# An encoder block on one core: 234 products on zeros in front of the opening, with moving rows read straight on, in turn from two or more places, at several distances and widths

## The chip, the cores and the metric

The kernel runs on one core of a Trainium2 chip. The metric is the device time of one execution in microseconds; the figure for a kernel is the median of its runs. Two runs of the kernel before took 1772.62 and 1772.77 us, a median of 1772.69 us.

## What is computed

One layer of a bidirectional encoder block on 256 tokens of 2048 channels, fp32, batch 1. Cut to what matters:

```
proj = h @ w_in                                # 2048 -> all inputs of the branches and gates
q, k, v, r, af, ab, hy_u, gate_logits = split(proj)
y_gla = gla_branch(q, k, v, r, af, ab, ...)    # chunked gated linear attention, both directions
y_hy = hyena_branch(hy_u, ...)                 # short conv, long filters from a small network, two gates
merged = g0 * (y_gla @ w_gla_o) + g1 * (y_hy @ w_hy_o)
h = layernorm(ALPHA * h + merged @ w_out)
h = layernorm(ALPHA * h + square(relu(h @ w_ff1)) @ w_ff2)
```

Nearly all of the work is products of the 256 tokens with large weight matrices, which are streamed from HBM once.

## The kernel before

Each weight block arrives as fp32 (a `raw` tile, 1 MB) and is split by `split_hi_lo` (L104, L105) into a high part, rounded by ScalarE, and a low part, the rest, by VectorE. Activations are split in the same way, so that a product of fp32 accuracy is made of three products of rounded parts (high by high, high by low, low by high). `channel_products` (L193, L197) keeps weights stationary and moves 512 columns (high and low part of the 256 tokens, side by side in memory) past the high weights, then 256 columns past the low ones. `token_half` (L250 to L252) and the MLP's second matrix (L1378 to L1380) keep activations stationary and move 512 columns of weights. The moving columns of each of these products lie next to each other in memory.

The kernel begins with the *opening*: the first five blocks of `w_in` and x itself come together in eleven pieces (`PIECES`, issued on SyncE's queue at L317), each is split on ScalarE and VectorE (L104, L105, L349, L352, L354), and TensorE takes it slice by slice of the contraction, 16 in all: five products of 512 columns (L337) and four of 256 (L339) each. In front of it `wu`, 512 columns of zeros, is written by VectorE (L310), and two fp32 products on it (L313, tile `warm`, four rows in the profile) keep TensorE at work until the first piece has been split. After the opening come the blocks of q and k, with the filter network's products (L425, L426, tile `mlp`) and the filters' transforms (L469 to L473, L378 to L382) between them, then the other projections, the branches, the output projection and the MLP.

The order of instructions on each engine is set by a scheduler that simulates a timeline of the whole program (`schedule_with_timeline_sim=True`); `tc.keep_in_program_order` pins an instruction to its place in the program's order. The filter work has no fixed place: it is put where the simulated timeline has room. Each engine works its queue in order.

The lines around the change:

```
wu = xp.tile([P, 512], F32, tag="wu", name="wu")
nc.vector.memset(wu, 0.0)
pw = psum_side("warm")
for _ in range(2):
    MM(pw, wu[:, 0:P], wu, start=True, stop=True)
```

Of the kernel before, what the change touches and what calls it, by code (L numbers as in the profile page):

```python
# [10 lines left out]
F32R = mybir.dt.float32r  # L11
# [5 lines left out]
P = 128  # L17
# [21 lines left out]
PIECES = tuple((k, 1) for k in range(6)) + tuple((k, 2) for k in range(6, KT, 2))  # L39

TWO_PI = 2.0 * math.pi
RED_C1 = 6.28125
RED_C2 = float.fromhex("0x1.fb4p-10")
RED_C3 = TWO_PI - RED_C1 - RED_C2
MAGIC = 1.5 * 2.0 ** 23
# [4 lines left out]
def block_kernel(  # L50
# [25 lines left out]
    nc = tc.nc  # L76
# [20 lines left out]
    def psum_main(name):  # L97
        return mmp.tile([P, 512], F32, tag="mm", name=name)

    def psum_side(name):  # L100
        return sdp.tile([P, 512], F32, tag="sd", name=name)

    def split_hi_lo(hi, lo, src):
        return (nc.scalar.copy(hi, src),  # L104
                nc.vector.tensor_tensor(lo, src, hi.bitcast(F32), op=ALU.subtract))  # L105
# [45 lines left out]
    def weight_half(n, h, by_channel=False):  # L151
        i = low_turn[0] % 3
        low_turn[0] += 1
        lo = (base, wp, wp)[i].tile([P, D // 2 + 8], F32R, tag=f"wlo{i}", bufs=1, name=f"wlo{n}_{h}")
        return (wp.tile([P, D // 2], F32R, tag="whi", bufs=3, name=f"whi{n}_{h}"),
                lo[:, 0:D // 2] if by_channel else lo[:, 8:])
# [140 lines left out]
    with tc.tile_pool(name="xp", bufs=1) as xp, tc.tile_pool(name="xq", bufs=1) as xq:  # L297
        def units(pool, tag, n, **kw):
            t = pool.tile([P, n, OPENING * P], F32R, tag=tag, name=f"open_{tag}", **kw)
            return lambda a, b: t[:, a:b].rearrange("p k (b j) -> p k b j", b=OPENING)  # L300

        pieces = {}
        for k0, n in PIECES[::-1]:
            if k0 < 10:
                pieces[k0] = xp.tile([P, n, KROW], F32, tag=f"xw{k0}", name=f"xw{k0}")
            else:
                raw = wp.tile([P, D], F32, tag="raw", bufs=3, name=f"xw{k0}")
                pieces[k0] = raw[:, 0:n * KROW].rearrange("p (k c) -> p k c", k=n)
        wu = xp.tile([P, 512], F32, tag="wu", name="wu")
        nc.vector.memset(wu, 0.0)  # L310
        pw = psum_side("warm")
        for _ in range(2):
            MM(pw, wu[:, 0:P], wu, start=True, stop=True)  # L313

        fetched[0] = OPENING
        for k0, n in PIECES:
            nc.sync.dma_start(pieces[k0], first[k0 * P:(k0 + n) * P, :].rearrange("(p k) c -> p k c", k=n))  # L317

        u_y, u_g, u_k, u_q, u_x = (units(base, "yT", 12), units(qp, "G", 6), units(qp, "k", 3), units(qp, "q", 2),
                                   units(xq, "sp", 3))  # L320
        places = {6: (u_y(6, 8), u_y(8, 10)), 8: (u_y(10, 12), u_g(0, 2)), 10: (u_g(2, 4), u_g(4, 6)),
                  12: (u_k(0, 2), u_q(0, 2))}
        for i in range(3):
            t = weight_half(-1, i, True)
            places[i] = [v[:, 0:OPENING * P].rearrange("p (k b j) -> p k b j", k=1, b=OPENING) for v in t]
            places[3 + i] = (u_y(2 * i, 2 * i + 1), u_y(2 * i + 1, 2 * i + 2))
        places[14], places[15] = (u_k(2, 3), u_x(0, 1)), (u_x(1, 2), u_x(2, 3))

        def part_of(kt, part):
            k0 = kt if kt in places else kt - 1  # L330
            return places[k0][part][:, kt - k0]

        def products(kts, b, part):
            for kt in kts:
                w = part_of(kt, part)[:, b]
                if part == 0:
                    MM(open_ps[b], w, xT[:, kt], start=(kt == 0), stop=(b == 0 and kt == KT - 1))  # L337
                elif b:
                    MM(open_ps[b][:, 0], w, xT[:, kt, 0], start=False, stop=(kt == KT - 1))  # L339

        turned = False
        for k0, n in PIECES:
            raw = pieces[k0]
            kts = range(k0, k0 + n)
            split_hi_lo(xT[:, k0:k0 + n, 0], xT[:, k0:k0 + n, 1], raw[:, :, 0:L])
            w = raw[:, :, L:].rearrange("p k (b j) -> p k b j", b=OPENING)

            def split(hi, lo, w, first=0):
                nc.scalar.copy(hi, w)  # L349
                if first == 0:  # L350
                    low = hi[:, :, 0, 96:]
                    nc.vector.tensor_tensor(low, w[:, :, 0, 96:], low.bitcast(F32), op=ALU.subtract)  # L352
                bs = slice(1 - first, None)
                nc.vector.tensor_tensor(lo[:, :, bs], w[:, :, bs], hi[:, :, bs].bitcast(F32), op=ALU.subtract)  # L354

            if k0 == 0:
                hi, lo = places[0]
                for bs in (slice(0, 3), slice(3, OPENING)):
                    split(hi[:, :, bs], lo[:, :, bs], w[:, :, bs], bs.start and 1)
            elif k0 == 14:  # L360
                for i in range(n):
                    split(places[k0 + i][0], places[k0 + i][1], w[:, i:i + 1])
            else:
                split(places[k0][0], places[k0][1], w)
            if k0 + n == KT:
                for b in range(OPENING):
                    for part in (0, 1):
                        products(kts, b, part)
            else:
                for part in (1, 0) if turned else (0, 1):  # L370
                    for b in range(OPENING):
                        products(kts, b, part)
                turned = not turned and k0 >= 6 and k0 < 12
# [42 lines left out]
    def filt_layer(l):  # L416
        def run():
            mw, mc, g = fst["mw"], fst["mc"], fst["g"]
            with tc.high_priority():
# [9 lines left out]
                n = fp.tile([P, L], F32, tag="ng", name=f"mlpn{l}")  # L429
                nc.vector.tensor_scalar(n, a, 1.0 / TWO_PI, MAGIC, op0=ALU.mult, op1=ALU.add)  # L430
                nc.vector.tensor_scalar(n, n, -MAGIC, None, op0=ALU.add)
                for cst in (RED_C1, RED_C2, RED_C3):
                    nc.vector.scalar_tensor_tensor(a, n, -cst, a, op0=ALU.mult, op1=ALU.add)
# [86 lines left out]
    for i in range(2 * NCH):  # L520
        c, o = divmod(i, 2)
        n = 4 + (i * 21) // 15
# [1021 lines left out]
    ps = psum_main("w2_33_0")  # L1544
# [38 lines left out]
    with tc.high_priority(), tc.issue_after(done.ins):  # L1583
        add_ff(pss[1][:, 0:256], 1, 1792, 256, last=True)
        mv = ep.tile([P, 2], F32, tag="mv", bufs=2, name="mvl")
        nc.vector.bn_aggr(mv, st2[:, 1])
        y, t, v, rs = (ep.tile([P, 1], F32, tag=f"fin{i}", name=f"fin{i}") for i in range(4))
# [160 lines left out]
```

## Time and profile before

| | |
|---|---|
| median of the runs | 1772.69 us |
| the profiled execution, its own time | 1773.26 us |
| its span, first to last instruction | 1771.4 us |
| mean granted TensorE clock | 0.999 |
| TensorE (PE) busy, instructions | 1763.8 us, 8771 |
| VectorE (DVE) busy | 1460.9 us |
| ScalarE (ACT) busy | 1048.4 us |
| DMA, mean over the span | 241 GB/s |

Times within the profile are counted from the start of the span. A row of the timeline gives start, length, engine, line, operation, output<-inputs, form and count; in brackets it has how long the engine was idle before and what ended that. A row of a group gives the count, then busy time and mean duration of one, then idle time before. PE's products overlap at their ends, so that a row's length is longer than the distance to the next start. PEld is TensorE's weight load, beside PE.

### The profile page before, as it was taken

To read this page: it belongs to the slowest core of one execution; us is meant where nothing else is said; L and a number is where in the kernel's file an instruction comes from. 1 tells how busy PE (TensorE), PEld (TensorE's weight loads), DVE (VectorE), ACT (ScalarE), POOL (GpSimd) and SP (SyncE) were. 2 spreads that over 40 slices of the span, in tenths; PEclk is the share of its full clock that TensorE was granted. 3 is DMA by queue.
4 is the path that set the end of the run, shared out by engine and by line. 5 is a ranking of instruction groups with operands and counts; after the bars stand their busy time and mean duration, and the time that the engine had idled before them with its cause. 6 is when DMAs were issued, how large, how long until landed. Compare 5 with 4: busy or idle time off the path is not lost.

```text
span 1771.4 us, 23597 instructions
## 1 busy us (share of the span) xinstructions
PE 1763.8 (100%) x8771; PEld 1490.0 (84%) x8771; DVE 1460.9 (82%) x1899; ACT 1048.4 (59%) x1446; POOL 186.5 (11%) x243
## 2 busy tenths in 40 slices
PE   9999999999999999999999999999999999999998
PEld 7888888888888888888888889888888888888886
DVE  6789996777688888888845558889999999999998
ACT  6587876787344444444444446666766666666653
POOL 1001111000110101021000000011111111111100
PEclk9999999999999999999999999999999999999999
DMA  8678888634796868797555664688878788888864
GB/s 329 230 252 265 290 258 257 199 141 173 262 299 222 279 232 273 232 287 256 192 192 187 264 247 165 207 267 253 258 242 277 241 251 256 269 249 247 267 207 168
DMA packets 87299, 427.13 MB, mean 241 GB/s; under 512 B 9800, under 2 KB 14296, under 8 KB 45584
## 3 DMA queue, kind: packets, MB, share of 16 engines
q1 hardware_dynamic: 47664, 336.35, 51.5%
q0 software_dynamic: 30560, 67.38, 18.3%
q10 hardware_dynamic: 8960, 21.89, 3.5%
q8 instruction: 69, 1.13, 0.3%
q14 instruction: 46, 0.38, 0.1%
HBM read 382.12 MB, written 12.06 MB: 223 GB/s over the span
## 4 chain that ended last, share of the span: by engine, by line
PE 96%; DVE 3%; issue 1%; ACT 0%; DVEq 0%
PE f L193 13%; PE f L197 6%; PE w L1379 5%; PE w L1380 5%; PE w L1378 5%; PE g L251 3%; PE g L252 3%; PE ux L251 3%; PE ux L252 3%; PE g L250 3%; PE ux L250 3%; PE k L193 2%; PE r L251 2%; PE r L252 2%; PE v L251 2%; PE v L252 2%
## 5 line engine op out<-in xcount | busy, mean ns | idle before, releaser
L104 ACT CAST whi<-raw 128x1024 fp32r<-128x1024 f32 x360 | 377.8, 1054 | 401.0 <-PE ux L252 86.7
L105 DVE TENSOR_TENSOR wlo<-raw,whi 128x1024 fp32r<-128x1024 f32 x360 | 438.2, 1222 | 158.1 <-ACT whi L104 154.2
L193 PE MATMUL f<-hT,whi 128*128 128x512 f32 x984 | 244.3, 391 | 0.0
L193 PEld LDWEIGHTS f<-hT,whi 128*128 128x128 f32 x984 | 180.2, 188 | 35.0
L1236 DVE TENSOR_TENSOR wlo<-fraw,whi 128x1024 fp32r<-128x1024 f32 x112 | 136.9, 1223 | 13.5 <-ACT whi L1239 9.8
L197 PEld LDWEIGHTS f<-hT,wlo 128*128 128x128 f32 x984 | 123.8, 188 | 5.2
L1239 ACT CAST whi<-ring 128x1024 fp32r<-128x1024 f32 x56 | 59.0, 1054 | 113.9 <-DVE ring L1236 113.9
L1299 POOL DMA_DIRECT2D ring<-wblk x56 | 48.6, 868 | 726.3 <-DVE ring L1236 719.9
L197 PE MATMUL f<-hT,wlo 128*128 128x256 f32 x984 | 124.9, 279 | 0.0
L1239 ACT CAST whi<-fraw 128x1024 fp32r<-128x1024 f32 x112 | 117.6, 1050 | 0.0
L1239 ACT CAST b_h<-ring 128x1024 fp32r<-128x1024 f32 x112 | 87.9, 834 | 22.3 <-PE w L1380 21.6
L251 PE MATMUL g<-wlo,xT 128*128 128x512 f32 x256 | 100.1, 391 | 0.0
L251 PE MATMUL ux<-wlo,xT 128*128 128x512 f32 x256 | 99.9, 390 | 0.0
L252 PE MATMUL ux<-whi,xT 128*128 128x512 f32 x256 | 99.9, 390 | 0.0
L252 PE MATMUL g<-whi,xT 128*128 128x512 f32 x256 | 99.8, 390 | 0.0
L250 PE MATMUL g<-whi,xT 128*128 128x512 f32 x256 | 92.2, 390 | 0.0
L250 PE MATMUL ux<-whi,xT 128*128 128x512 f32 x256 | 89.2, 389 | 0.0
L1236 DVE TENSOR_TENSOR ring<-ring 128x512 f32<-128x512 f32 x112 | 77.2, 689 | 1.9
L1236 DVE TENSOR_TENSOR b_l<-ring,b_h 128x1024 fp32r<-128x1024 f32 x56 | 68.4, 1222 | 8.1 <-ACT b_h L1239 8.0
L1236 DVE TENSOR_TENSOR wlo<-ring,whi 128x1024 fp32r<-128x1024 f32 x56 | 68.6, 1225 | 2.1 <-ACT whi L1239 0.3
L1236 DVE TENSOR_TENSOR fa<-ring,fa 128x1024 fp32r<-128x1024 f32 x56 | 68.3, 1220 | 0.0
L1300 POOL DMA_DIRECT2D ring<-ring x56 | 67.2, 1201 | 0.0
(529 smaller groups left out, 4257.8 us busy)
## 6 DMA issues: line engine op xcount, KB each, us to landing
raw<-wblk SPq DMA_DIRECT2D x188, 1024.0 KB, 5.1
fraw<-wblk SPq DMA_DIRECT2D x56, 1024.0 KB, 4.9
ring<-wblk SPq DMA_DIRECT2D x56, 1024.0 KB, 7.0
ring<-wblk POOLq DMA_DIRECT2D x56, 256.0 KB, 4.4
ring<-ring POOLq DMA_DIRECT2D x56, 256.0 KB, 5.2
conv_sb<-conv_rows SPq DMA_DIRECT2D x12, 1024.0 KB, 8.7
w<-w4s ACTq DMA_DIRECT2D x16, 512.0 KB, 5.1
Td<-T POOLq DMA_DIRECT2D x32, 256.0 KB, 5.3
```

The costliest lines, as they stand in the source:

```text
L104: return (nc.scalar.copy(hi, src), nc.vector.tensor_tensor(lo, src, hi.bitcast(F32), op=ALU.subtract))
L105: nc.vector.tensor_tensor(lo, src, hi.bitcast(F32), op=ALU.subtract))
L193: MM(ps[:, :, ts], hi[:, js], act[:, kt, :, ts], start=(kt == 0 and opens), stop=(kt == KT - 1))
L197: MM(ps[:, 0, ts], lo[:, js], act[:, kt, 0, ts], start=False, stop=False)
L250: order(MM(pss[tb], sh, wh, start=(kt == ends[0]), stop=False))
L251: order(MM(pss[tb], sh, wl, start=False, stop=False))
L252: order(MM(pss[tb], sl, wh, start=False, stop=(kt == ends[1])))
L1236: return pin(nc.vector.tensor_tensor(dst, a, b, op=op))
L1239: return pin(nc.scalar.copy(hi, src))
L1378: pin(MM(ps, sh, wh, start=(p == begin), stop=False))
L1379: MM(ps, sh, wl, start=False, stop=False)
L1380: pin(MM(ps, sl, wh, start=False, stop=(p == end - 1)))
```

## The change

A new function, `side_by_side`, is called between the two products of the warm-up and the opening. It makes a tile `both` of 2560 fp32 columns (rounded form) in the pool `xq`, fills it with zeros by five ScalarE copies of `wu`, and issues 38 groups of products on it: two groups with plain moving rows, 35 forms, and one more plain group. A group has six products, the three last forms (two kinds of rows by turns) eight. All write the bank of the warm-up, each opens and closes its own sum, and all are pinned in program order. Nothing reads what they write.

```
+def side_by_side(tc, nc, pool, ps, zero):
+    both = pool.tile([P, 2560], F32R, tag="both", name="both")
+    for i in range(5):
+        tc.keep_in_program_order(nc.scalar.copy(both[:, i * 512:(i + 1) * 512], zero))
+
+    def st(d, n=P, step=1, first=1536):
+        at = first - d // 4
+        return both[:, at:at + n * step].rearrange("p (a b) -> p a b", b=step)[:, :, 0]
+
+    def rows(n, apart, count=2):
+        t = both[:, 0:512 * 2]
+        if apart * count >= n:
+            return t[:, 0:apart * count].rearrange("p (a b) -> p b a", a=count)[:, 0:n]
+        return both[:, 0:n * count].rearrange("p (a b) -> p b a", a=count)
+
+    mv = both[:, 0:512]
+    kinds = [mv] + [rows(256, s) for s in (256, 264, 288, 320, 384, 512)]
+    kinds += [mv.rearrange("p (h a b) -> p h b a", h=2, a=2), rows(128, 128, 4), rows(64, 64, 8),
+              mv.rearrange("p (a b c) -> p b a c", a=2, c=2), mv.rearrange("p (a b c) -> p b a c", a=2, c=4),
+              mv.rearrange("p (a b c) -> p b a c", a=2, c=8)]
+    forms = [[(st(0), m)] for m in kinds]
+    two = rows(256, 256)
+    forms += [[(st(d), two)] for d in range(32, 256, 32)]
+    forms += [[(st(0, 64), two)], [(st(0, step=2), two)]]
+    low = rows(128, 128)
+    forms += [[(st(d), low)] for d in range(0, 256, 32)]
+    forms += [[(st(0), rows(128, 256))], [(st(0), mv[:, 0:256])]]
+    halves = kinds[7]
+    forms += [[(st(0), two), (st(0), low)], [(st(0), halves), (st(0), low)], [(st(32), two), (st(32), low)]]
+    for form in [[(st(0), mv)]] * 2 + forms + [[(st(0), mv)]]:
+        for i in range(8 if len(form) > 1 else 6):
+            s, m = form[i % len(form)]
+            tc.keep_in_program_order(
+                nc.tensor.matmul(ps[0:s.free_size(), 0:m.free_size()], s, m, start=True, stop=True))
+
...
         for _ in range(2):
             MM(pw, wu[:, 0:P], wu, start=True, stop=True)
+        side_by_side(tc, nc, xq, pw, wu)
```

`st(d)` are the stationary 128 columns, which begin d bytes ahead of column 1536 (64 columns wide in one form, every second column in another). `rows(n, apart, count)` takes one word from each of `count` places that lie `apart` words from each other, then the next word of each, and so on: n x count columns. The counts, by how the moving row is read:

| moving row | products of 512 columns | products of 256 columns |
|---|---|---|
| straight on (`mv`) | 24 | 6 |
| two, four or eight neighbours, then from the other half (`c=2`, 4, 8) | 6, 6, 6 | |
| single words in turn from two places | 108 | 66 |
| single words in turn from four and from eight places | 6, 6 | |
| sum | 162 | 72 |

The instruction counts are the same apart from that; the scheduler's simulated timeline, and with it the order of the filter work, has changed. Three places follow. First the start of PE's queue, before and now; `warm` is the bank of the warm-up, `open_91` to `open_95` the sums of the opening, `whi-1_0` the high part of its first weights:

```order
L313 MATMUL warm<-wu 128x512 x2
L337 MATMUL open_91<-xT,whi-1_0_135 128x512
L337 MATMUL open_92<-xT,whi-1_0_135 128x512
L337 MATMUL open_93<-xT,whi-1_0_135 128x512
L337 MATMUL open_94<-xT,whi-1_0_135 128x512
```

```order
L350 MATMUL warm<-wu 128x512 x2
L77 MATMUL warm<-both 128x512 x132
L77 MATMUL warm<-both 64x512 x6
L77 MATMUL warm<-both 128x512 x6
L77 MATMUL warm<-both 128x256 x60
...
L77 MATMUL warm<-both 128x512 x6
L375 MATMUL open_91<-xT,whi-1_0_375 128x512
L375 MATMUL open_92<-xT,whi-1_0_375 128x512
```

The 234 products stand between the warm-up and the opening's first product, which was second in the queue before; the dots stand for the 24 products of the three mixed forms.

Then the start of ACT's queue, before and now; `xT` is the high part of x, `xw_112` the first piece:

```order
L104 ACT_TABLE_LOAD
L104 CAST xT<-xw_112 128x256
L349 CAST whi-1_0_135<-xw_112 128x384
L349 CAST whi-1_0_135<-xw_112 128x256
L104 CAST xT<-xw_111 128x256
```

```order
L47 ACT_TABLE_LOAD
L47 CAST both<-wu 128x512 x5
L141 CAST xT<-xw_112 128x256
L387 CAST whi-1_0_375<-xw_112 128x384
L387 CAST whi-1_0_375<-xw_112 128x256
L141 CAST xT<-xw_111 128x256
```

The five copies into `both` stand in front of the first split; the rest of the opening's splits keep their order.

Last the place in PE's queue, behind the opening, where the first layer of the filter network (`mlp`, its input `gx`) stands between the products of q, before and now:

```order
L193 MATMUL q_0_701<-xT,whi_0_533 128x512 x8
L197 MATMUL q_0_701<-xT,wlo_0_532 128x256 x8
L197 MATMUL q_0_701<-xT,wlo_1_536 128x256 x8
L193 MATMUL q_0_701<-xT,whi_1_537 128x512 x3
L425 MATMUL mlp_388<-gx_385,mlp_ws 128x256
L193 MATMUL q_0_701<-xT,whi_1_537 128x512 x5
L193 MATMUL q_1_797<-xT,whi_0_632 128x512 x7
L426 MATMUL mlp_388<-gx_385,mlp_ws 128x256
```

```order
L230 MATMUL q_0_941<-xT,whi_0_773 128x512 x8
L234 MATMUL q_0_941<-xT,wlo_0_772 128x256 x7
L463 MATMUL mlp_628<-gx_625,mlp_ws 128x256
L234 MATMUL q_0_941<-xT,wlo_0_772 128x256
L234 MATMUL q_0_941<-xT,wlo_1_776 128x256 x5
L464 MATMUL mlp_628<-gx_625,mlp_ws 128x256
L234 MATMUL q_0_941<-xT,wlo_1_776 128x256 x3
L230 MATMUL q_0_941<-xT,whi_1_777 128x512 x8
```

The two products of the network's first layer have moved forward, from the last quarter of this block and the one behind it into its second and third quarter, and stand closer to each other.

## The prediction

> **What bounds the kernel now.** I read the page first, then the waits of PE, then PE's timeline of the opening. The page:
>
> ```profile
> span 1771.4 us, 23597 instructions
> PE 1763.8 (100%) x8771; PEld 1490.0 (84%) x8771; DVE 1460.9 (82%) x1899; ACT 1048.4 (59%) x1446; POOL 186.5 (11%) x243
> PEclk9999999999999999999999999999999999999999
> PE 96%; DVE 3%; issue 1%; ACT 0%; DVEq 0%
> ```
>
> PE is busy over the whole span, at the full granted clock, and is 96% of the chain that ended last. A busy PE could still hide short gaps, so the second view asks what PE waited for:
>
> ```profile
> engine line waited for: us in total, times, longest us
> PE warm L313 <- DVE ones_sb L375: 1.5, 1, 1.5
> PE w L251 <- DVE wr L105: 0.3, 1, 0.3
> PE w L250 <- DVE zr L1236: 0.3, 1, 0.3
> PE lo L1598 <- DVE fin L1592: 0.2, 1, 0.2
> ```
>
> That is the whole list: 1.5 us before PE's first product and 0.8 us later. There is no pocket of waiting in which added products could disappear, and none that a PE arriving later would find already over. The third view is PE's timeline (start, length, line, out<-in, form, count):
>
> ```profile
> 1.50 3.78 PE L313 MATMUL warm<-wu 128*128 128x512 f32 x4 [1.50 <-DVE ones_sb L375]
> 4.93 2.50 PE L337 MATMUL open<-xT,whi-1_0_135 128*128 128x512 f32 x5
> 7.23 0.80 PE L339 MATMUL open<-xT,wlo-1_0_134 128*128 128x256 f32 x4
> 8.06 1.42 PE L337 MATMUL open<-xT,whi-1_1_137 128*128 128x512 f32 x5
> ...
> 11.41 1.31 PE L337 MATMUL open<-xT,open_yT 128*128 128x512 f32 x5
> ...
> 16.30 2.46 PE L337 MATMUL open<-xT,open_yT 128*128 128x512 f32 x10
> ...
> 32.49 1.99 PE L193 MATMUL q<-xT,whi 128*128 128x512 f32 x8
> 34.32 2.03 PE L197 MATMUL q<-xT,wlo 128*128 128x256 f32 x16
> 36.19 3.82 PE L193 MATMUL q<-xT,whi 128*128 128x512 f32 x16
> 39.85 2.03 PE L197 MATMUL q<-xT,wlo 128*128 128x256 f32 x16
> ```
>
> Products overlap at their ends, so the price of one is the distance between starts. Sixteen products of 512 columns take 39.85 - 36.19 = 3.66 us, **0.229 us each**; sixteen of 256 take 36.19 - 34.32 = 1.87 us, **0.117 us each**. The opening runs from 4.93 to 32.49, 27.56 us for sixteen slices of the contraction. Three slices in its middle take 16.30 - 11.41 = 4.89 us, 1.63 us each, so sixteen would take 26.1 us. The missing 1.5 us lies at its start: the first five products stand 0.46 us apart ((7.23 - 4.93) / 5), and the second slice waits a little for its splitting.
>
> **The change, part by part.** It adds 234 products to PE between the warm-up (L313) and the first product of the opening (L337), all on zeros and all into the bank of the warm-up: 162 of 512 moving columns and 72 of 256. Nothing that the kernel needs depends on them, but PE works in order, so the whole opening stands behind them. ACT gets five copies of 128x512 in front of its first split. No DMA is added and none removed.
>
> *Where the added products start.* These rows carry it (ACT's, then the last split of the opening on DVE):
>
> ```profile
> 0.74 1.28 ACT L104 ACT_TABLE_LOAD   x1 [0.74 <-PEq L1740]
> 3.84 0.41 ACT L104 CAST xT<-xw 128x256 fp32r<-128x256 f32 x1 [1.81 <-DMA xw<-first]
> 13.63 0.62 ACT L104 CAST xT<-xw 128x512 fp32r<-128x512 f32 x1 [1.15 <-DMA xw<-first]
> 24.73 0.69 DVE L354 TENSOR_TENSOR open_sp<-xw,open_sp 128x512 fp32r<-128x512 f32 x1
> ```
>
> The table load ends at 2.02 and a copy of this size takes 0.62 us, so the fourth of the copies, which holds the first weights, ends at about 4.5, and the fifth at 5.1. The warm-up holds PE until about 4.93 anyway: the products start there, with no new wait. The first split of x goes from 3.84 to 5.1, 1.3 us late. I cost that at nothing: its cover is the added products, more than 40 us of them. Without that cover it would cost the 1.3 us.
>
> *The part whose price is known.* If every column came at the price of the rows above, the sum is 162 x 0.229 + 72 x 0.117 = 37.1 + 8.4 = 45.5 us. The five slow products at the start of dense work are now five of the added ones: 5 x (0.46 - 0.229) = 1.2 us more. The opening behind them finds its first splits done and gives back its 1.5 us. **Net +45.2 us.**
>
> *The part whose price is not in the trace.* Every product of the kernel before reads its moving columns from adjacent words. Of the added ones 186 do not: 120 of 512 columns and 66 of 256 take one word here, the next one 256 to 2048 bytes further on, and so on in turn. Of the rest, 24 of 512 and 6 of 256 read straight on, and 18 of 512 take two, four or eight neighbours before they jump; those I price as adjacent (for the six with two neighbours that is a guess worth 1.2 us at most). For the price of a jump I bound by the other engines that take fp32 words from the same memory, from the groups of the first 33 us (last number before the second bar: mean ns of one):
>
> ```profile
> L104 ACT CAST whi<-raw 128x1024 fp32r<-128x1024 f32 x3 | 3.1, 1049 | 3.8 <-PE open L339 2.0 <-DMA raw<-wblk 1.9
> L104 ACT CAST xT<-xw 128x256 fp32r<-128x256 f32 x6 | 2.4, 406 | 4.1 <-DMA xw<-first 3.8
> L105 DVE TENSOR_TENSOR wlo<-raw,whi 128x1024 fp32r<-128x1024 f32 x3 | 3.6, 1223 | 3.4 <-ACT whi L104 3.4
> L105 DVE TENSOR_TENSOR xT<-xw,xT 128x256 fp32r<-128x256 f32 x6 | 2.5, 422 | 4.7 <-ACT xT L104 4.7
> ```
>
> From 256 to 1024 words ACT takes (1049 - 406) / 768 = 0.84 ns a word, DVE (1223 - 422) / 768 = 1.04 ns. PE takes one in 0.229 / 512 = 0.45 ns, about half of ACT's. The lower bound is that a jump costs PE nothing: 0.229 and 0.117 stay. The middle bound is ACT's pace: 0.43 us for 512 columns and 0.215 for 256. The upper one is DVE's: 0.534 and 0.267. (That a jump should help is the last rival.) I take ACT's pace. PE is the only engine of the trace that takes more than one word in 0.84 ns, and in every row that shows it the words are neighbours; where nothing can come along with a word, the fastest pace at which any row here takes words is ACT's. The extra is 120 x (0.43 - 0.229) + 66 x (0.215 - 0.117) = 24.1 + 6.5 = 30.6 us.
>
> [...]
>
> *Behind the opening.* Scheduling by a simulated timeline has also moved rows of the filter work. The earliest place where PE could wait for it is the first layer of the filter network:
>
> ```profile
> 46.25 0.41 DVE L423 TENSOR_TENSOR gx<-emb_sb,gx 64x256 fp32r<-64x256 f32 x1
> 47.94 0.28 PE L425 MATMUL mlp<-gx,mlp_ws 128*128 128x256 f32 x1
> ```
>
> Before, the low part of its input is ready 14.2 us after the opening's end at 32.49, and the first product comes at 15.4 us. Now the first product stands about 13.6 us of PE work behind that end and the second, which alone needs the low part, at 14.5. DVE's row for the low part has moved up too. What is queued behind is the rest of the q and k products, so a wait here would count in full; I put it at 0, with 1 us either way. Everything later keeps its distance from the opening: weight splits wait for buffers that PE frees, and so shift with it.
>
> **The sum.** Net +45.2 and +30.6 make +75.8 us. The span goes from 1771.4 to 1847.2. The profiled execution took 1773.26 us, so 1849.1 for it; the median of the runs is 0.57 us lower, 1772.69, which gives **1848.5 us**.
>
> **The rivals.**
>
> *A jump costs nothing* (24%), or the rows do not jump on the chip as they do in the code. PE then takes every column in 0.45 ns: +45.2, **1817.9 us**. For it speaks that no row shows an engine losing anything to a pattern of addresses; against it that PE's pace is twice ACT's and has never been seen without neighbours.
>
> *Only some jumps cost* (13%): the price hangs on the distance between the two places, or on how many are read in turn, and about half of the 186 products pay. 45.2 + 15.3 = +60.5, about **1833 us**. For it speaks only that distances can differ in what they collide with; the trace has no row for or against.
>
> *A jump costs more than a word at DVE's pace* (9%): three of PE's steps a column, 0.69 us for 512 and 0.35 for 256, extra 55.3 + 15.4 = 70.7, in all +115.9, about **1889 us**. Nothing in the trace takes words that slowly, which is why it is small.
>
> *Two places are read at once* (3%). This is the one that ends on the other side: two streams in turn would bring two columns per step, 0.115 and 0.058 us. The jumping products would save 120 x 0.114 + 66 x 0.059 = 17.6 us against 45.2, leaving +27.6, **1800.3 us**, which is within 2%. It decides once the 234 products and what hangs on them cost under 35.4 us, 2% of 1772.69. Against it: in the q products above, PE reads neighbours at 0.45 ns and gains nothing from lying side by side; nothing goes faster.
>
> **How the numbers follow.** The forecast has 51%; with the five cases that is 100%. The range 1814 to 1867 takes in the forecast, free jumps (1817.9), the half case (1833) and DVE's pace (120 x 0.305 + 66 x 0.15 = 46.5 instead of 30.6, so 1864.4), with some 3 us for waits that the new order could bring or take; left out are the dearest and the cheapest case, 12%. About 2%, or 35 us, can be told from no change here. Faster by over 2%: 0, since added work has no wait to remove. Within 2%: 0.03, the last rival. Slower by over 2%: 0.97, the rest.
>
> **What would show it.** In PE's timeline the added products form one piece on L77 that starts at about 4.9 us; it should last about 77 us by the forecast, 47 if jumps are free, 62 by the half case. Inside it the first products after the slow five should stand 0.23 us apart, the ones that take two words in turn 0.43, those with four or eight neighbours 0.23 again, and weights at other distances should change little. ACT's first split should come at about 5.1 us without PE noticing, and the opening should take 26.1 us instead of 27.6. Were the difference in time far from the length of that piece, the argument that nothing hides it would be wrong; were the piece 77 us with the loss in other groups than the jumping ones, the price would be right for a wrong reason.

## The result and the profile after

The changed kernel takes 1819.71 us (median of 1819.09 and 1820.33), against 1772.69 before: 47.0 us more, a ratio of 1.0263 (95% interval 1.0238 to 1.0288). It is slower by over 2% and inside the range, but 29 us below the predicted 1848.5 and close to the 1817.9 us of the first rival, by which a jump costs nothing.

PE's timeline of the changed kernel, cut to the warm-up, the added piece, the opening's first products and the first of q (start, length, line, out<-in, form, count):

```profile
1.50 3.78 PE L350 MATMUL warm<-wu 128*128 128x512 f32 x4 [1.50 <-DVE ones_sb L413]
4.29 47.78 PE L77 MATMUL warm<-both 128*128 128x512 f32 x234
51.91 1.31 PE L375 MATMUL open<-xT,whi-1_0_375 128*128 128x512 f32 x5
53.06 0.63 PE L377 MATMUL open<-xT,wlo-1_0_374 128*128 128x256 f32 x4
...
77.88 1.99 PE L230 MATMUL q<-xT,whi 128*128 128x512 f32 x8
```

The piece lasts from 4.29 to 51.91, 47.6 us, where 77 were forecast and 47 is the free-jump case. The opening follows without a wait and takes 77.88 - 51.91 = 25.97 us (26.1 predicted, 27.56 before), its first five products now 0.23 us apart. The end of the opening has moved from 32.49 to 77.88, by 45.4 us; from there to the end of the span it is 1817.0 - 77.88 = 1739.1 us, against 1771.4 - 32.49 = 1738.9. So the whole difference is made before the first product of q, and nothing is given back behind it. PE's waits say the same:

```profile
PE warm L350 <- DVE ones_sb L413: 1.5, 1, 1.5
PE g L288 <- DVE wlo L142: 1.0, 1, 1.0
PE w L288 <- DVE wr L142: 0.3, 1, 0.3
PE w L287 <- DVE zr L1274: 0.3, 1, 0.3
```

One wait of 1.0 us, in the gates, is all that the new order brought; the first layer of the filter network, named as a risk, has none. ACT's first split came at 4.64 us instead of 5.1 (five copies back to back took 2.69 us, not 3.1), and nobody waited for it:

```profile
2.04 2.69 ACT L47 CAST both<-wu 128x512 fp32r<-128x512 f32 x5
4.64 0.40 ACT L141 CAST xT<-xw 128x256 fp32r<-128x256 f32 x1
```

Inside the piece the prices are not what any of the cases said. The rows below are stretches of the changed kernel, each from the first start of one set of groups to the first start of the next. After the two ends stand the stretch in us, PE's busy time and count, the granted clock, the DMA's share and its GB/s; the count includes the last product of the set before, and here and there one more, which reach in:

```profile
6.75:9.46 2.72, 2.72 (x13) 1.00 1.04 401
9.46:18.53 9.06, 9.06 (x43) 1.00 1.02 423
18.53:20.22 1.69, 1.69 (x7) 1.00 0.98 402
20.22:23.22 3.00, 3.00 (x7) 1.00 0.35 85
23.22:25.20 1.98, 1.98 (x7) 1.00 1.03 418
25.20:28.17 2.97, 2.97 (x13) 1.00 0.95 367
28.17:39.83 11.66, 11.66 (x55) 1.00 0.24 93
39.83:45.86 6.03, 6.03 (x55) 1.00 0.00 0
45.86:46.59 0.73, 0.73 (x8) 1.00 0.00 0
```

| reading of the moving row | products | us each |
|---|---|---|
| straight on, 512 columns | 12 | 0.227 |
| single words from two places in turn, seven kinds | 42 | **0.216** |
| from four places | 6 | 0.282 |
| from eight places | 6 | 0.500 |
| pairs of neighbours from two places | 6 | 0.330 |
| four and eight neighbours | 12 | 0.248 |
| two places, weights at seven distances, 64 wide, every second column | 54 | 0.216 |
| two places, 256 columns | 54 | 0.112 |
| straight on, 256 columns | 6 | 0.122 |

Jumping at every word between two places is not dearer than reading straight on but **cheaper**, by 11 ns of 227, at each distance tried. What is dearer are more places (0.282 and 0.500), and, against what the prediction guessed, pairs (0.330). The cheaper and the dearer readings nearly cancel, and so the sum comes out at the free-jump case.

### The profile page after: what moved, and what is told of

Read it like the earlier page. It is cut to its first block, busy times and chain, and to the rows that moved or that the text cites. A ratio compares the mean times of both kernels' runs of the same rounds, so it can differ in the third digit from the quotient of the medians.

```text
span 1817.0 us, 24068 instructions
## 1 busy us (share of the span) xinstructions
PE 1808.5 (100%) x9005; PEld 1528.1 (84%) x9005; DVE 1460.1 (80%) x1899; ACT 1051.4 (58%) x1451; POOL 186.5 (10%) x243
## 4 chain that ended last, share of the span: by engine, by line
PE 95%; DVE 4%; ACT 1%; issue 1%; DVEq 0%
PE f L230 12%; PE f L234 6%; PE w L1418 5%; PE w L1416 5%; PE w L1417 5%; PE ux L288 3%; PE ux L289 3%; PE ux L287 3%; PE g L288 3%; PE g L289 3%; PE g L287 3%; PE warm L77 3%; PE k L230 2%; PE r L288 2%; PE uv L289 2%; PE ho L287 2%
```

## The experiments

Theory A, formed on these rows: PE fetches the even and the odd columns by two ways (or two columns at a time), and each way wants neighbours within its own run of words. Two places in turn give each way a straight run of its own; straight rows give each way every second word; pairs make each way jump. Theory B: straight rows lose their 11 ns to the weight load beside them. Theory C: a way keeps the last two lines, and only a jump to a third one costs. All three are guesses; no trace shows a way or a line, which is the theories' word for a group of neighbouring words.

### How rows are read (e1_readers)

The same kernel with other forms in `side_by_side`:

```
+    def every(k, n=512):        # one place, every k-th word
+        return both[:, 0:n * k].rearrange("p (a b) -> p a b", b=k)[:, :, 0]
...
+    def near(k):                # two places k words apart, run by run of 2k
+        return both[:, 0:512].rearrange("p (g a b) -> p g b a", a=2, b=k)
...
+    far = both[:, 0:2048].rearrange("p (w i j) -> p i j w", w=2, j=4)
+    kinds += [far[:, 0:128, 0:2], far[:, :, 0]]   # two places, two or one word of each four
...
+    forms += [(st(64), mv), (st(32), mv), (st(step=2), mv), (st(32), two), (st(step=4), two)]
```

> The added products again, 39 groups of six on zeros, with other readings; nothing else is changed. In the changed kernel two places in turn stood 216 ns apart, straight rows 227, four places 283, eight places 487, pairs from two places 328. Theory A: PE fetches even and odd columns by two separate ways, and each way wants neighbours in its own run. Then two places in turn take 216 at any distance from four words on (4, 8, 16, 32, 64, 257, 258), also where only two words of each four are used; two words apart (0, 2, 1, 3) stays near 227, since both ways share a line; every second word, or every fourth from two places, leaves each way one word a line and takes 280 or more; and straight rows keep 227 with 64 and 32 stationary columns. Theory B: straight rows lose their 11 ns to the weight load, which walks the same memory at the same pace. Then straight rows fall to about 221 with 64 and 219 with 32 stationary columns and change with the distance of the weights, and short distances (4, 8 words in turn) stay at 227. Theory C: each jump to another line costs, unless the line is one of the last two. Then every second to fourth word cost about what pairs cost, and all two-place readings 216.

The run took 1831.02 us. Stretches of it, cut in the same way:

```profile
7.76:9.12 1.36, 1.36 (x7) 1.00 1.06 416
9.12:10.42 1.30, 1.30 (x8) 1.00 1.04 430
10.42:13.11 2.69, 2.69 (x8) 1.00 1.01 424
13.11:15.80 2.69, 2.69 (x7) 1.00 1.01 418
15.80:18.57 2.77, 2.77 (x8) 1.00 1.03 427
18.57:19.98 1.41, 1.41 (x8) 1.00 0.95 391
19.98:29.04 9.06, 9.06 (x43) 1.00 0.78 284
29.04:30.81 1.77, 1.77 (x7) 1.00 0.93 393
30.81:32.21 1.40, 1.40 (x8) 1.00 0.10 41
32.21:34.86 2.65, 2.65 (x7) 1.00 0.00 0
36.48:37.87 1.39, 1.39 (x8) 1.00 0.00 0
37.87:40.57 2.70, 2.70 (x7) 1.00 0.00 0
43.41:46.18 2.77, 2.77 (x13) 1.00 0.00 0
47.58:48.87 1.29, 1.29 (x7) 1.00 0.00 0
```

In this order they are (the last column is explained below):

| reading of the moving row, 512 columns | us each | words that the even columns take of each four |
|---|---|---|
| straight on | 0.227 | 2 |
| two places, 256 words apart | 0.217 | 4 |
| every second word; every third | 0.448; 0.448 | 1 |
| every fourth word | 0.462 | 1 |
| two words apart (0, 2, 1, 3) | 0.235 (0.229 over the last five) | 2 |
| 4, 8, 16, 32, 64, 257 and 258 words apart, 42 products | 0.216 | 4 |
| six places | 0.295 | |
| four places, 171 words apart | 0.233 | |
| pairs from four places | 0.442 | |
| two places, two words used of each four | 0.232 | 2 |
| two places, one word used of each four | 0.450 | 1 |
| straight on, 64 and 32 stationary columns | 0.231 | 2 |
| two places, 32 stationary columns | 0.215 | 4 |

Theory B falls: with a quarter of the weights to load, straight rows are no faster (0.231 against 0.227), and with the weights 8 to 56 words further on they stay at 0.230 to 0.234. Theory C falls: it has every two-place reading at 0.216, and two of them took 0.232 and 0.450; it has every second word at the price of pairs, 0.33, and it took 0.448.

Theory A missed one of its cases too: two words used of each four should have taken 0.216 and took 0.232. The readings of single words from one and two places fall into groups by another count. Take the even columns of a product of 512 (the odd ones read in the same way), and count how many words they take of each four neighbouring words that they come to. Four, because between places two and four words apart the price changed: 0.235 (0.229 over the last five) and 0.216. With one word of four (every second to fourth word, and one word used of each four) a product took 0.448 to 0.462 us; with two (straight on, two apart, and two words used of four) 0.227 to 0.235; with all four (four apart and more) 0.215 to 0.217. One of four means 256 such groups, and 0.450 / 256 is **1.76 ns a group**. At that price the 128 groups of two of four make 225 ns, measured 0.227 to 0.235, and the 64 groups of all four make 113 ns, but no reading here took less than 0.215 us. The prices are measured; the 1.76 ns is an estimate from the reading with one word used of four, and how PE fetches its columns is not shown. Straight rows are also less steady than this count says: in the last third of this run they took 0.230 to 0.238, the dearest with the row begun one word later, while two places with 32 stationary columns stayed at 0.216. What moves them is open. The count covers neither pairs nor four places, where 128 words apart had taken 0.282 and 171 words apart took 0.233.

### Many places (e8_many_places)

This run was made to settle that. Four, six and eight places and pairs, each at several distances, in place of the forms above:

```
...
+    def pairs(apart):
+        return both[:, 0:2 * apart].rearrange("p (w i) -> p w i", w=2)[:, :, 0:256].rearrange("p w (i j) -> p i w j", j=2)
...
+    forms = [(st(), turns(d, 128, 4)) for d in (128, 129, 130, 131, 132, 136, 144, 160, 192, 256)]
+    forms += [(st(), pairs(d)) for d in (256, 257, 258, 260, 264, 272, 288, 320, 384, 512)]
```

> The added products once more, 38 groups on zeros, all but three of them with four, six or eight places in turn or with pairs from two places, at several distances. By the first run of readings, a way of PE that opens a new line for each word needs 450 ns for 512 columns, and four places 128 words apart took 283, 171 words apart 232. Theory D (two places collide when a way's distance between them is near a multiple of 1024 bytes): of four places, 128 to 132 words apart and 256 words apart are slow (280 or more), 136 to 192 fast (near 230); of pairs, 256 to 264 and 512 slow (330), 272 to 384 fast. Theory F (what counts is that both places of a way cross into a new line at the same time): 128, 130, 132, 136, 144, 160, 192 and 256 are all slow, since a way's distance is then whole lines, and 129 and 131 are fast, near 230; of pairs, 257 and 258 are fast and the rest slow.

The run took 1851.59 us. Two of its stretches, four places 128 and 129 words apart, six products each:

```profile
8.94:10.61 1.66, 1.66 (x7) 1.00 1.05 431
10.61:12.01 1.41, 1.41 (x7) 1.00 1.02 429
```

As the median distance between starts, four places took 235 ns at 129 words apart and 234 at 131, and 271 to 283 at all the other distances. So for four places the prices fall as theory F said and not as D did: dear at the eight even distances, 234 and 235 ns at the two odd ones. What makes them so is not shown. For pairs neither is right: 327 to 335 ns at all ten distances, 257 and 258 among them. Six places took 296 to 312. Eight took 434 to 498, and neither theory says anything of them. In all of these the even columns, and the odd ones, come back to a group of four words that they have taken from before. Four and six places, pairs, and four of the ten distances with eight places cost less than the 450 of one word used of each four. Whether the coming back makes the difference stays open. It hardly touches the result, in which these readings are 18 of 234 products.

### The change with straight rows only (e2_straight)

```
             s, m = form[i % len(form)]
+            m = both[:, 0:m.free_size()]
```

> The change with every moving row read straight on: the same 234 products, counts, widths and weights, and no jump. Theory A (the change costs the number of its products at the straight price, and reading in turn adds about nothing): 162 x 0.227 + 72 x 0.117 = 45.2 us for the piece without its cold start, 1818 to 1820 us in all. Rival (the jumps are a good part of the 47 us): under 1810 us.

1818.93 us, and in its timeline the piece lasts from 4.29 to 51.47:

```profile
4.29 47.35 PE L78 MATMUL warm<-both 128*128 128x512 f32 x234
51.47 1.30 PE L376 MATMUL open<-xT,whi-1_0_375 128*128 128x512 f32 x5
```

That is 47.2 us, against 47.6 with all the jumps. What the change costs is the number of its products at the straight price; how they read adds 0.4 us in all (0.6 without the first six products, which were slower by 0.2 us here).

### The token products in turn (e3_token_in_turn)

If the 11 ns are real, the kernel before loses them at nearly every product. Here the weights of the token products are stored as evens, then odds, and read in turn, so that the sums lie as before:

```
+    def by_turns(ap):
+        return ap.rearrange("p (a b) -> p b a", a=2)
...
-            wh = hi[:, j * 512:(j + 1) * 512]
+            wh = read(hi[:, j * 512:(j + 1) * 512])     # read=by_turns
...
+    def in_turn(w):              # how the weights are laid out in HBM
+        return w.reshape(*w.shape[:-1], -1, 256, 2).swapaxes(-1, -2).reshape(w.shape)
```

> The kernel before, with no added products. The weights of the token products (the projections r, v, the gates, u and the three output matrices but for the last quarter of the last) are stored with each 512 columns as evens, then odds, and read from the two halves in turn, so that the sums come out in the same order as before. Nothing is left out. 1248 x 3 products change their reading. Theory A (reading from two places in turn saves 11 ns of 227, with real numbers as with zeros): 3744 x 0.011 = 41 us less, about 1731 us. Rival 1 (the gain was that of zeros, or of weights that never change): 1772 us. Rival 2 (something else takes the place of PE: VectorE is over 90% busy in parts): between 1735 and 1765, with PE waiting for the splits.

1736.09 us (1735.62 to 1742.32), ratio 0.9805 (0.9785 to 0.9824): 36.4 us less, of 41 expected. It is faster, though the interval leaves open whether by 2%. A stretch in which almost nine of ten products are token products, in the kernel before and here:

```profile
600.00:700.00 100.00, 100.00 (x447) 1.00 0.80 263
```

```profile
600.00:700.00 100.00, 100.00 (x466) 1.00 0.86 275
```

19 products more in the same 100 us; the token products among them stand 0.216 us apart, against 0.227. Real numbers and weights that change gain as zeros do, and rival 1 falls. Of the missing 5 us, 2.4 are new waits of PE for splits, the second rival in small:

```profile
PE g L254 <- DVE wlo L105: 0.8, 3, 0.4
PE v L254 <- DVE wlo L105: 0.7, 2, 0.6
PE uv L254 <- DVE wlo L105: 0.5, 1, 0.5
PE r L254 <- DVE wlo L105: 0.4, 1, 0.4
```

Where the rest went is open.

### The MLP's second matrix too (e4_second_matrix)

```
+            wh, wl = by_turns(wh), by_turns(wl)
             pin(MM(ps, sh, wh, start=(p == begin), stop=False))
...
-    quad = quad.transpose(0, 2, 1, 3, 4).reshape(n2, 2, P, D)
+    quad = in_turn(quad.transpose(0, 2, 1, 3, 4).reshape(n2, 2, P, D))
```

> The token products in turn (1736.09 us) and the 1176 products of the MLP's second matrix too; the products with stationary weights read straight on again. Nothing is left out. Theory A (11 ns a product, as long as VectorE keeps up): 1176 x 0.011 = 13 us less, about 1723 us, with little waiting of PE in the MLP. Rival (VectorE is the bound of the MLP as soon as PE gets any faster): 1730 us or more.

1726.76 us, ratio 0.9742 (0.9727 to 0.9756): 9.3 us less than the run before it, of 13 expected. In the MLP itself, from the first product of the second matrix to the last of the first, it took 562.3 us against 573.1, so 10.8 of the 13; 1.9 us were lost ahead of it, where PE waited longer for the splits of v (2.1 us against 0.7). So theory A holds in the main. The rival's bound does not show yet, since PE hardly waits in the MLP:

```profile
1200.00:1300.00 100.00, 99.85 (x527) 1.00 0.86 262
1400.00:1500.00 100.00, 100.00 (x528) 1.00 0.85 262
```

### Most products in turn (e5_most_in_turn)

Also the products with stationary weights, whose moving rows are then the two halves of the tokens in turn; the sums come out token by token, and their readers follow:

```
-                MM(ps[:, :, ts], hi[:, js], act[:, kt, :, ts], start=(kt == 0 and opens), stop=(kt == KT - 1))
+                MM(ps[:, :, ts], hi[:, js], both(act[:, kt]), start=(kt == 0 and opens), stop=(kt == KT - 1))
...
+        both = (lambda t: t.rearrange("p l (a b) -> p l b a", a=2)) if turned else lambda t: t[:, :, ts]
...
-        halves = [a.rearrange("p (t j) -> p t j", j=P) for a in (ps[:, 0], low)]
+        halves = [a.rearrange("p (j t) -> p t j" if turned else "p (t j) -> p t j", j=P) for a in (ps[:, 0], low)]
```

> As in the run of the token products, and also the second matrix of the MLP (1176 products of 512 columns), and the products with stationary weights in the opening, q, k and the MLP's first matrix, whose moving rows are then the two halves of the tokens in turn (about 1230 products of 512 and as many of 256 columns; the reading of their sums changes order with them). Nothing is left out. Theory A: 41 us as there, 1176 x 0.011 = 13, 1230 x 0.011 = 13.5 and 1230 x 0.006 = 7 us more, about 1698 us. Rival 1 (only zeros gain): 1772. Rival 2 (PE is no longer the bound): the part of the MLP, where VectorE is 93% busy, gives little, and the time stays above 1715 us with PE waiting for VectorE there.

1717.21 us (1714.94 to 1720.61), ratio **0.9689** (0.9675 to 0.9703): 55 us faster than before, but 19 short of theory A. Its own mark for rival 2 was a time above 1715 us with PE waiting for VectorE in the MLP, and that is what came. PE's waits, and a stretch of the MLP (after the length: PE, PEld, DVE, ACT and POOL busy):

```profile
PE f L195 <- DVE sum_fr L1240: 3.2, 4, 0.9
PE f L195 <- DVE dftl_fr L1240: 2.7, 5, 0.7
PE v L254 <- ACT whi L104: 2.2, 1, 2.2
PE v L255 <- DVE wlo L105: 1.7, 4, 0.6
```

```profile
1400.00:1500.00 100.00, 98.34 (x528) 86.72 (x527) 95.18 (x122) 66.96 (x89) 17.57 (x20) 1.00 0.85 262
```

528 products in these 100 us are as many as in the run with the second matrix alone, where PE did not wait: the products are faster, and the gain turned into waits, mostly for VectorE, which is busy for 95.2% of this stretch. From the first product of the second matrix to the last of the first it takes 557.8 us (1100.6 to 1658.4), against 562.3 in the run with the second matrix (1105.2 to 1667.5). The 896 products of 512 and 896 of 256 columns in it should have saved 896 x 0.011 + 896 x 0.005 = 14 us, so 9.5 of the 19 were lost here; 5 and 4 had been missing in the two runs before. The price itself held: over the whole trace the products in turn stand 0.216 us apart where PE does not pause. Its pauses (starts over a third further apart than the price) come to 31 us in all, against 12 in the kernel before, and that is what theory A is short of.

### Sums read on, written in turn (e6_sums_read_on)

In the last run the addition that reads the sums of the MLP's first matrix reads both of its inputs two words apart, the sums in PSUM and the low part that ACT has copied out. It takes 481 ns, against 422 before (first the kernel before, then the last run, groups of 1150 to 1650 us):

```profile
L1236 DVE TENSOR_TENSOR dfth_fr<-f,f_l 128x256 f32<-128x256 f32 x20 | 8.4, 422 | 2.4 <-ACT f_l L1239 2.2
L1240 DVE TENSOR_TENSOR dfth_fr<-f,f_l 128x256 f32<-128x256 f32 x20 | 9.6, 481 | 1.3 <-ACT f_l L1243 1.1
```

Turned round:

```
+            dst = dst.rearrange("p t j -> p j t")
+            halves = [a.rearrange("p (j t) -> p j t", j=P) for a in halves]
```

> As the run with most products in turn (1717.21 us), but the sums of the MLP's first matrix are read by VectorE in the order in which they lie in PSUM, and written to the two halves in turn, instead of read in turn and written on. Nothing is left out. Theory A (the 481 ns of that addition there, against 422 in the kernel before, come from reading PSUM two words apart, and PE waits for them): back to about 422 ns, and 2 to 6 us less in all, 1711 to 1715 us. Rival (writing in turn costs as much, or PE's waits hang on the rest of VectorE's work): 1716 to 1719 us.

Theory A's price was wrong: written in turn, the addition takes longer still, in the same stretch of time:

```profile
L1240 DVE TENSOR_TENSOR dfth_fr<-f,f_l 128x256 f32<-128x256 f32 x20 | 12.5, 624 | 1.3 <-ACT f_l L1243 1.1
```

And the time stays: 1717.78 us, ratio 0.9695 (0.9679 to 0.9711). 143 ns more per addition moved it by less than the runs spread. The same part of the MLP, in the last run and here (after the length: PE, PEld, DVE, ACT and POOL busy):

```profile
1100.64:1658.43 557.79, 550.26 (x2956) 487.07 (x2955) 528.76 (x667) 379.64 (x507) 96.58 (x110) 1.00 0.84 257
1096.83:1656.05 559.21, 550.78 (x2956) 486.98 (x2955) 534.05 (x667) 379.28 (x507) 96.78 (x110) 1.00 0.84 257
```

VectorE is busy 5.3 us longer and the part takes 1.4 us more. So the length of this addition does not set PE's waits, and VectorE's amount of work does so only in part. PE's waits still end at VectorE's writes to `sum_fr` and `dftl_fr` (5.9 us in the last run, 7.0 here). That they hang on the rest of VectorE's work, as the rival says, fits and is not shown; what times those writes stays open.

## Why the prediction was right and where it was wrong

**No cover for the added products: right.** The list of PE's waits carried it. The piece of 47.6 us stands in full in the time, and the two spans agree to 0.2 us behind the opening.

**The range: right by its width.** The time lies in it because the range takes in free jumps. At the forecast's own price the piece would have lasted 77 us, so the range says nothing for that price.

**The known part, +45.2 us: right in its sum, by luck in one term.** The end of the opening moved by 45.4, and by 44.95 with straight rows alone (to 77.44). The opening behind the piece takes 25.97 us (26.1). The first six added products took 6.75 - 4.29 = 2.46 us, 1.1 more than six at 0.227, where 1.2 was forecast for slow products. But the first one's record starts at 4.29, only 0.07 us after the last of the warm-up's four, and those stand 0.85 us apart. So about 0.8 of the 1.1 us is the end of the warm-up, and slow products cost some 0.3 (both are estimates from the single starts). How long the slow start lasts changed from run to run: full pace came at 5.2 us in the run of the readers, at 7.6 in that of many places.

**The price of a jump: the step that failed.** The forecast took ACT's 0.84 ns a word, since PE's pace "has never been seen without neighbours". But ACT's rows read neighbours too, and bound nothing about jumps; and two places in turn are not without neighbours, since each place is read straight on. The 174 products with two places cost 0.216 and 0.112 us, less than the lower bound of 0.229 and 0.117, where the term had 0.43 and 0.215. Of +30.6 us, 0.4 to 0.6 came, by the run with straight rows. The 12 products with four and eight places are dearer than straight ones (0.282 and 0.500, on average 0.39 against the 0.43 charged), and the pairs, priced as adjacent, cost 0.330.

By the count of the readers' run, one word of each four for the even columns cost 0.450 us for 512 columns, two 0.227 to 0.235 and all four 0.215 to 0.217. What the prediction missed is that one word here and one there can still be all four of each four for the even columns, and all four for the odd ones, as it is in the 174 products with two places. The products in turn stand 0.216 us apart, the straight ones 0.227.

**Weights at other distances change little: right.** 0.216 at all seven distances, for two places.

**The rivals.** Free jumps, at 24%, came nearest, by luck: some readings do have a price (0.282, 0.330 and 0.500 against 0.227), and cheaper and dearer readings cancel in the sum. "Only some jumps cost" had the right shape and the wrong share. The last one, two places at once, pointed the right way with a tenth of the size: 11 ns saved, not 114.

## What to carry to other kernels

When dense products have stopped waiting, look at how their moving rows are read: at fp32 width, reading straight on cost 0.227 us for 512 columns and reading two places in turn 0.216, 4.8% less. Laying out the weights as evens, then odds gave it without any work on the chip and brought this kernel from 1772.5 to 1726.8 us. Reading the activations in turn as well brought it to 1717.2, with dearer additions on VectorE (481 ns against 422). Four places (0.232 to 0.283 us) and pairs (0.33) were dearer than straight rows. Expect an engine as full as VectorE was in the MLP before, at 93%, to take back part of the gain: of 14 us expected there from the activations, 9.5 did not come. To price single words read from one or two places, count how many words of each four the even columns take, and the odd ones, not how far apart two consecutive words lie: one of four took 0.450 us here, two 0.227 to 0.235, all four 0.215 to 0.217. For pairs and for more places this count did not hold here.

## What the runs showed of the hardware

- A product of 512 fp32 columns took 0.216 us from two places in turn at every distance tried from 4 to 512 words, 0.227 to 0.238 straight on, and 0.45 to 0.46 with every second to fourth word. One of 256 columns took 0.112 from two places and 0.117 to 0.122 straight on.
- Four places took 0.271 to 0.283 us at the eight even distances tried, from 128 to 256 words, and 0.232 to 0.235 at the three odd ones, 129, 131 and 171.
- Stationary columns that are every fourth word slowed products from two places to 0.237 us (median of six starts); with every second word, 64 or 32 columns they stayed at 0.215 to 0.216.
- VectorE's addition of 256 columns, one input in PSUM, took 422 ns straight on, 481 reading both inputs two words apart and 624 writing to two places 512 bytes apart in turn.
